# Index scores summed from the PSUM bank of their logits, and a bisection step written as a tensor-scalar operation

## The chip, the cores and the metric

The kernel runs on one core of one Trainium2 chip. The metric is device microseconds (us) of one execution, as the median of several runs. Engines are named as the profile names them: PE (matmul) and PEld (its weight loads), DVE (VectorE), ACT (ScalarE), POOL (GpSimd), SP (SyncE, which issues most DMAs).

## What is computed

Two blocks follow each other on 1024 tokens of 1024 channels. Block 1 has two layers of a hybrid of a spatial gating unit and a sparse attention; block 2 is a windowed attention with a convolution and a mixture of experts. The change touches the sparse attention of block 1 alone, where each query takes the 256 keys with the largest index score:

```python
logits = jnp.einsum('bthd,bsd->bths', qib, k_idx) * (IDX_DIM ** -0.5)     # 8 index heads
score = jnp.einsum('bth,bths->bts', wb, jax.nn.relu(logits)).astype(jnp.float32)
score = jnp.where(causal[None], score, -jnp.inf)
_, idx = lax.top_k(score, top)                                            # top = 256
valid = idx <= qpos[None, :, None]
...
sc = jnp.einsum('bthd,btkd->bthk', qb, k_sel).astype(jnp.float32) * attn_scale
p = jax.nn.softmax(jnp.where(valid[:, :, None, :], sc, -jnp.inf), axis=-1)
```

## The kernel before

The 1024 queries are eight tiles of 128. Tiles 0 and 1 see at most 256 keys and need no choice. For tile i from 2 to 7 the function `select(i)` works on n = 128 (i + 1) keys and writes a bias of 0 or -1e30 for each query and key, which the attention adds to its logits. It has these stages:

- **Scores** (lines 622 to 638). For each of the 8 index heads, and for each of one or two parts of w_ = 384, 512, 320 or 448 keys, PE computes the logits with two matmuls into a PSUM bank of the kind "sm" (L629), ACT rectifies and scales them into an SBUF tile `rel` (L632), and DVE multiplies by the head's weight and adds to the scores `sc` in SBUF (L635 for the first head, L637 for the others). That is 80 such pieces in each layer, 160 in all.
- **Bisection** (L646 to L665). The upper halves of the scores are taken as 16-bit integers `up`. In 15 steps the threshold `cand`, one number for each partition, is found: a count of the keys at or above it (L607), a comparison of the count with K (L662), and the new threshold (L664).
- **Choice** (L668 to L721): lower halves of the scores, ties, and the bias.

Two streams of such tiles run beside each other: (2, 4, 6) and (3, 5, 7). So in each layer there are three bursts of scores, of tiles 2 and 3, of 4 and 5, and of 6 and 7, with bisections between and behind them. They are generators that `bg` places between the steps of the dense products, which keep PE busy meanwhile (the columns for v, u, q, z_a and z_b; `dense_nat`, L100 to L102). What is emitted is put in order by the Tile scheduler, which gives each engine one fixed queue. The queues are worked off strictly in that order, so an instruction that waits holds everything behind it on its engine.

Where tiles live matters here. The bank plan in this stage gives the kind "sm" two PSUM banks, which index logits, the spatial gating products and others take in turn. `rel` has the tag "r2" of the SBUF pool `tmp`, which has seven places that `rel` shares with `up`, `junk`, `lw`, `eq`, `pre` and parts of the modulation rows. A place or a bank is given again when the last reader of its old content is done.

Other work in these stages that the prediction speaks of: the weights of the dense products are split into a high part by ACT (L108, `whi`) and a low part by POOL (L111, `wlo`); POOL also normalizes v for the spatial gate (L798, L799: one multiplication and one addition for each tile of tokens, both with two SBUF inputs) and applies the rotary embedding (L518 to L523). The modulation rows are summed on DVE (L465).

Of the kernel before, what the change touches and what calls it, by code (L numbers as in the profile page):

```python
# [10 lines left out]
FT = mybir.dt.float32  # L11
# [8 lines left out]
OP = mybir.AluOpType  # L20
# [8 lines left out]
BIG = 1e30  # L29
SL = 96          # tokens of one expert's block  # L30
NE = 32
PSUM = bass.MemoryType.PSUM
# [8 lines left out]
def tile_hybrid(ctx, tc, I, out):  # L41
# [7 lines left out]
    banks = {}  # L49
    psum2 = ctx.enter_context(tc.tile_pool(name="psum2", bufs=2, space=PSUM))  # L50

    def bank_plan(big, half, sm, tr, sc=0):
        """Banks of PSUM: big tiles of two, the others of one. Two small and two transposed ones stay in place."""
        if banks:
            banks["stack"].close()
        st = ExitStack()
        banks.update(stack=st, pool=st.enter_context(tc.tile_pool(name="psum", bufs=2, space=PSUM)),
                     big=big, half=half, sm=sm, tr=tr, sc=sc, turn={"sm": 0, "tr": 0})
# [54 lines left out]
    # weights are streamed two 128-row blocks at a time and split one step ahead of their use  # L113
# [11 lines left out]
    # the number of stages whose loads wait for an instruction, and which  # L125
# [33 lines left out]
    # background work, placed between the steps of a product. Generators in bgs yield about the time they take.  # L159
    # Streams hold the vector engine's long chains: they yield the time they take there and whether what comes next  # L160
    # starts on the tensor engine, which then must not come up before the chain is done. now is the tensor engine's
    # time so far, dve that up to which the vector engine has work.
# [97 lines left out]
    def dense_T1(KT, rhs, evac, bgt=1300.0):  # L260
        """One block of 128 channels: the halves take turns so that two banks last."""
# [29 lines left out]
    # every streamed weight, in the order of use  # L291
# [20 lines left out]
    # ------------------------------------------------------------------ block 1  # L312
# [9 lines left out]
    # rotary tables  # L322
# [29 lines left out]
    # modulation rows  # L352
# [13 lines left out]
    # first layer: scale and shift as columns, and h straight into its transposed halves. The products for 256 channels  # L366
    # of one of them are summed over row blocks by the vector engine, by the two slow ones or by the tensor engine.
# [77 lines left out]
    # later modulation rows: products summed over row blocks by the vector engine, over rows by one product with ones  # L445
# [63 lines left out]
    def rope(dst, src, t, H, eng):  # L509
        """Rotary embedding of H heads of 64 channels; t is one tile, or None for all tiles with one head each."""  # L510
# [48 lines left out]
    def layer(l, xin, hT=None):  # L559
# [6 lines left out]
        # keys, values, index keys and index weights  # L566
# [22 lines left out]
        # index queries  # L589
# [20 lines left out]
        def select(i):  # L610
            """Bias of query tile i: 0 at its 256 largest index scores, first ones on ties, else -BIG."""
# [11 lines left out]
            for g in range(2):  # L623
                for j in range(4):
                    h = 2 * j + g
                    for p in range(npart):
# [4 lines left out]
                        rel = tmp.tile([128, 512], FT, name="rel", tag="r2", bufs=7)  # L631
# [10 lines left out]
            # upper halves of the scores as integers: they rise with the scores where these are non-negative and fall  # L642
            # where they are negative. With fewer than 256 non-negative scores the threshold is the (n - 255)-th from the
            # most negative one, and all non-negative ones count as larger.
# [14 lines left out]
            for b in range(14, -1, -1):  # L659
# [4 lines left out]
                V.scalar_tensor_tensor(c2, x, 2.0 ** (b - 1) if b else 0.0, cand, op0=OP.add, op1=OP.add)  # L664
                cand = c2  # L665
                yield 360.0 + .52 * n, False, 0.0, 0.0
            # lower halves of the scores that share the threshold's upper half; of these the K2-th largest, if among the
            # eight largest  # L668
# [29 lines left out]
        def choose(sc, gt, c, cand, z, eq=None, pre=None):  # L698
            """The 256 scores above the threshold with halves cand and c, first ones where equal."""
# [24 lines left out]
        def recheck(tiles):  # L724
            """Tiles with a threshold beyond the eight largest lower halves: these by bisection."""
# [38 lines left out]
        # spatial gating: v, u  # L764
# [7 lines left out]
        def sgu():  # L772
# [3 lines left out]
            # causal spatial weights, transposed  # L776
# [53 lines left out]
        # a unit's probabilities take one place of 1024, or two where there are more than 512 keys  # L830
# [88 lines left out]
        # queries  # L919
# [11 lines left out]
        # z_a: X = 2 * u * spatial gate * silu(z_a)  # L931
# [10 lines left out]
        # z_b, transposed  # L942
# [25 lines left out]
        # half the gate over alpha, and the weights of the output product  # L968
# [49 lines left out]
        def fin2(t, ya, yb, rt):  # L1018
# [11 lines left out]
            # the norm of alpha * x + gate * y, all over alpha  # L1030
# [66 lines left out]
    # ------------------------------------------------------------------ block 2  # L1097
# [53 lines left out]
    def kv_prep():  # L1151
        """Values in two parts; keys with RMS norm and rotary embedding, doubled in X[:, :, 1, 256:512], transposed."""
# [135 lines left out]
    # short convolution on transposed channels  # L1288
# [31 lines left out]
    # gated merge, transposed: M = (1 + tanh) * projection, summed over both branches  # L1320
# [55 lines left out]
    # residual, second norm, router logits  # L1376
# [15 lines left out]
    # routing of one tile of tokens at a time: the two experts of each token, their gates, and the place of each  # L1392
    # assignment in its expert's list; assignment (k, token) is row 1024 k + token of Y
# [36 lines left out]
    def route(t, lg):  # L1430
# [45 lines left out]
        # gates  # L1476
# [7 lines left out]
        # slot + 1 in two exact parts, gate in three exact parts  # L1484
# [294 lines left out]
```

## Time and profile before

| | |
|---|---|
| median of 3 runs | 2515.39 us (2513.58 to 2515.87) |
| span of the profiled execution | 2515.2 us |
| busy: PE, PEld | 2194.3 us (87%), 1914.9 us (76%) |
| busy: DVE | 1705.0 us (68%) |
| busy: ACT, POOL | 1035.8 us (41%), 1301.4 us (52%) |
| scores and bisection of layer 1 | from 132 to about 500 us |
| scores and bisection of layer 2 | from 807 to about 1140 us |

The profile is of one execution, and the page gives its span, from the first instruction to the last; the metric's median is 0.2 us longer than it. The shares of busy time are averages over stages with different limits. The two stretches in the last rows are where the changed lines run, and they are read by themselves below. A duration is that of one instruction on its engine, and it includes what the instruction waits once it has begun; idle time before an instruction is shown with what ended it. "PEclk" is the clock granted to PE, 1.00 being the upper of its two levels.

### The profile page before, as it was taken

How to read it: one execution, taken by the hardware profiler on the slowest of the kernel's cores; microseconds unless marked ns; L12 is line 12 of the kernel's file. 1: busy time of each engine (PE TensorE's matmuls, PEld its weight loads, DVE VectorE, ACT ScalarE, POOL GpSimd, SP SyncE). 2: the span in 40 equal slices, each digit the busy share in tenths (PEclk: the TensorE clock that was granted, in tenths of full speed). 3: DMA queues.
4: the chain of work that ended last, by engine and by line, in shares of the span. 5: the costliest groups of instructions: out<-in, count | busy, mean ns of one | idle time of the engine just before them, and what ended most of it. 6: DMA issues, size and time to landing. Idle time of an engine off the chain costs nothing. (4 is left out here: it accounts for less than half of the span.)

```text
span 2515.2 us, 36403 instructions
## 1 busy us (share of the span) xinstructions
PE 2194.3 (87%) x13235; PEld 1914.9 (76%) x13235; DVE 1705.0 (68%) x3475; ACT 1035.8 (41%) x1875; POOL 1301.4 (52%) x1102
## 2 busy tenths in 40 slices
PE   5997888699989898877998999999998977887885
PEld 5897886488779898766786988888886767776774
DVE  8689889877745879896786268730103357887885
ACT  4233333455532342435564346631212125554554
POOL 4755473456737525725553355432335137776775
PEclk9998999699999899988999999999999989998998
DMA  7522112211123111122211111121211649887893
GB/s 225 181 79 80 50 34 75 90 55 64 39 72 112 37 53 36 58 88 73 73 42 42 39 38 30 30 79 50 64 46 53 234 169 300 265 293 248 272 292 62
DMA packets 146509, 265.51 MB, mean 106 GB/s; under 512 B 23672, under 2 KB 100880, under 8 KB 134016
## 3 DMA queue, kind: packets, MB, share of 16 engines
q1 hardware_dynamic: 139136, 241.99, 29.6%
q0 software_dynamic: 7168, 20.98, 4.0%
q8 instruction: 105, 1.72, 0.3%
q14 instruction: 100, 0.82, 0.1%
HBM read 228.83 MB, written 38.29 MB: 106 GB/s over the span
## 5 line engine op out<-in xcount | busy, mean ns | idle before, releaser
L111 POOL TENSOR_TENSOR wlo<-wraw,whi 128x512 fp32r<-128x512 f32 (+1 forms) x188 | 254.3, 1353 | 490.8 <-ACT whi L108 472.8
L101 PE MATMUL big<-wlo,s 128*128 128x256 f32 (+1 forms) x1536 | 441.2, 289 | 12.8 <-POOL wlo L111 12.8
L100 PE MATMUL big<-whi,s 128*128 128x256 f32 (+1 forms) x1536 | 439.2, 289 | 11.4 <-ACT s L506 8.8
L102 PE MATMUL big<-whi,s 128*128 128x256 f32 (+1 forms) x1536 | 440.9, 289 | 0.0
L101 PEld LDWEIGHTS big<-wlo,s 128*128 128x128 f32 x1536 | 300.1, 196 | 17.8 <-POOL wlo L111 15.2
L100 PEld LDWEIGHTS big<-whi,s 128*128 128x128 f32 x1536 | 296.7, 195 | 18.9 <-ACT s L506 11.2
L102 PEld LDWEIGHTS big<-whi,s 128*128 128x128 f32 x1536 | 299.5, 195 | 2.8 <-issue 0.9
L108 ACT ACTIVATE whi<-wraw 128x512 fp32r<-128x512 f32 (+1 forms) x188 | 117.8, 628 | 419.6 <-PE big L102 143.4
L111 DVE TENSOR_TENSOR ew<-s,ew 128x1024 fp32r<-128x1024 f32 x91 | 209.1, 2321 | 16.9 <-POOL ew L106 9.6
L607 DVE TENSOR_SCALAR_CACHE_REDUCE junk<-up,cand 128x512 bf16<-128x512 int16 (+5 forms) x192 | 179.7, 936 | 1.4
L101 PE MATMUL sm<-ew,xT 128*96 128x256 f32 x512 | 153.8, 300 | 30.3 <-DVE ew L111 25.1
L637 DVE SCALAR_TENSOR_TENSOR s<-rel,widx,s 128x384 f32<-128x384 f32 (+3 forms) x140 | 132.4, 970 | 50.6 <-ACT rel L632 49.9
L102 PE MATMUL sm<-ew,xT 128*96 128x256 f32 x512 | 152.6, 298 | 4.2 <-DVE xT L1627 3.6
L100 PE MATMUL sm<-ew,xT 128*96 128x256 f32 x512 | 152.8, 299 | 0.5 <-ACT ew L108 0.5
L100 PE MATMUL half<-s,whi 128*128 128x512 f32 x320 | 133.1, 416 | 17.9 <-DVE s L950 11.0
L632 ACT ACTIVATE rel<-sm 128x384 f32<-128x384 f32 (+3 forms) x160 | 80.9, 524 | 159.6 <-PE sm L629 105.7
L111 POOL TENSOR_TENSOR ew<-s,ew 128x1024 fp32r<-128x1024 f32 x47 | 130.9, 2792 | 25.3 <-ACT ew L108 18.8
L101 PE MATMUL half<-s,whi 128*128 128x512 f32 x320 | 131.5, 411 | 0.0
L102 PE MATMUL half<-s,wlo 128*128 128x512 f32 x320 | 129.9, 410 | 0.3 <-POOL wlo L111 0.3
L108 ACT ACTIVATE ew<-s 128x1024 fp32r<-128x1024 f32 x116 | 115.5, 1049 | 22.5 <-PE sm L102 11.5
L101 PEld LDWEIGHTS sm<-ew,xT 128*96 128x96 f32 x512 | 89.9, 176 | 40.6 <-DVE ew L111 32.3
L862 POOL TENSOR_SCALAR Z<-Z,rc 128x128 f32<-128x128 f32 (+7 forms) x88 | 63.2, 730 | 109.1 <-DVE rc L860 74.6
(628 smaller groups left out, 6306.9 us busy)
## 6 DMA issues: line engine op xcount, KB each, us to landing
wraw<-in_w_in_dram SPq DMA_DIRECT2D x164, 256.0 KB, 2.9
adaw<-in_w_ada_dram SPq DMA_DIRECT2D x48, 512.0 KB, 4.1
s<-in_w_gate_e_dram SPq DMA_DIRECT2D x23, 1024.0 KB, 4.8
s<-in_w_up_e_dram SPq DMA_DIRECT2D x23, 1024.0 KB, 7.2
s<-in_w_down_e_dram SPq DMA_DIRECT2D x23, 1024.0 KB, 9.2
X<-in_w_gate_e_dram SPq DMA_DIRECT2D x9, 1024.0 KB, 6.7
X<-in_w_up_e_dram SPq DMA_DIRECT2D x9, 1024.0 KB, 6.8
X<-in_w_down_e_dram SPq DMA_DIRECT2D x9, 1024.0 KB, 8.6
```

What stands on the lines that cost most here:

```text
L100: T.matmul(o, lh, rh, start=start, stop=False, skip_group_check=True)
L101: T.matmul(o, lh, rl, start=False, stop=False, skip_group_check=True)
L102: T.matmul(o, ll, rh, start=False, stop=stop, skip_group_check=True)
L108: A.activation(hi, src, AF.Copy)
L111: return (sub or V).tensor_tensor(lo, src, hi.bitcast(FT), op=OP.subtract)
L607: V.tensor_scalar(junk[:, :src.shape[1]], src, thr, 0.0, op0=op, op1=OP.add, accum_out=cnt)
L632: A.activation(rel[:, :w_], ps[:, :w_], AF.Relu, scale=0.125)
L637: V.scalar_tensor_tensor(d, rel[:, :w_], widx[:, i, h:h + 1], d, op0=OP.mult, op1=OP.add)
L862: G.tensor_scalar(P[hh][:, :n], P[hh][:, :n], rc[:, hh:hh + 1], 1.0, op0=OP.mult, op1=OP.mult)
```

## The change

Two lines of `select` are changed. All else in the diff are comments and docstrings that fall away, with blank lines in their place, so that the line numbers stay.

```diff
                             T.matmul(ps[:, :w_], qT[g][:, j, :], kist[a][:, p * w_:(p + 1) * w_], start=a == 0,
                                      stop=a == 1)
-                        rel = tmp.tile([128, 512], FT, name="rel", tag="r2", bufs=7)
+                        rel = ps
                         A.activation(rel[:, :w_], ps[:, :w_], AF.Relu, scale=0.125)
                         d = sc[:, p * w_:(p + 1) * w_]
...
                 V.tensor_scalar(x, cnt, K[:, 0:1], -float(2 ** b), op0=OP.is_lt, op1=OP.mult)
                 c2 = small1.tile([128, 1], FT, name=f"cand{z}")
-                V.scalar_tensor_tensor(c2, x, 2.0 ** (b - 1) if b else 0.0, cand, op0=OP.add, op1=OP.add)
+                V.tensor_scalar(c2, x, 2.0 ** (b - 1) if b else 0.0, cand[:, 0:1], op0=OP.add, op1=OP.add)
                 cand = c2
```

With the first, ACT writes the rectified logits over the logits in their PSUM bank, and DVE reads them there (L635, L637); `rel` takes no SBUF place any more, and the bank is given again only when DVE has read it. With the second, the old threshold enters as a scalar for each partition instead of a second tensor of one element; the arithmetic is the same.

Since buffers decide when the scheduler may place an instruction, the queues are ordered anew. Three places:

POOL in layer 1, around the normalization of v, before (`wlo` are low parts of weights that the dense product waits for, `X` the values of v, `vg` the gain and bias):

```order
L111 TENSOR_TENSOR wlo_2923<-wraw_2920,whi_2922 128x512
L798 TENSOR_TENSOR X_79<-X_79,vg_2756 128x512 x8
L799 TENSOR_TENSOR X_79<-X_79,vg_2756 128x512 x2
L781 AFFINE_SELECT ws_2761<-ws_2761 128x1024
L799 TENSOR_TENSOR X_79<-X_79,vg_2756 128x512
L111 TENSOR_TENSOR wlo_3136<-wraw_3133,whi_3135 128x512
```

and in the changed kernel:

```order
L111 TENSOR_TENSOR wlo_2875<-wraw_2872,whi_2874 128x512
L798 TENSOR_TENSOR X_79<-X_79,vg_2708 128x512 x8
L111 TENSOR_TENSOR wlo_3088<-wraw_3085,whi_3087 128x512
L799 TENSOR_TENSOR X_79<-X_79,vg_2708 128x512 x2
L781 AFFINE_SELECT ws_2713<-ws_2713 128x1024
```

The next low part of weights stands directly behind the eight multiplications now, ahead of three additions and the masking of the spatial weights.

PE in layer 1, at the end of the burst of tiles 4 and 5, before (`sm` are the logits' banks, `kist` the index keys, `qT` the index queries, `big` a dense product):

```order
L629 MATMUL sm_2603<-kist0_767,qT1_2377 128x384
L629 MATMUL sm_2603<-kist1_768,qT1_2377 128x384
L100 MATMUL big_3132<-whi_3273,s32_225 128x256
L101 MATMUL big_3132<-wlo_3274,s32_225 128x256
L102 MATMUL big_3132<-whi_3273,s32_226 128x256
L100 MATMUL big_3132<-whi_3273,s32_225 128x256
```

and in the changed kernel:

```order
L629 MATMUL sm_2504<-kist0_767,qT1_2361 128x384
L629 MATMUL sm_2504<-kist1_768,qT1_2361 128x384
L629 MATMUL sm_2509<-kist0_767,qT1_2330 128x320
L629 MATMUL sm_2509<-kist1_768,qT1_2330 128x320
L629 MATMUL sm_2514<-kist0_767,qT1_2361 128x384
L629 MATMUL sm_2514<-kist1_768,qT1_2361 128x384
```

Ten pieces of logits follow each other with nothing between them at this place now; before, dense matmuls stood between most of them.

DVE in layer 1, at the start of the burst of tiles 6 and 7, before (`s4` are the scores, `eq`, `pre`, `bias` the choice of tile 5):

```order
L710 TENSOR_SCALAR need1_3542<-cnt1_3540 128x1
L716 SCALAR_TENSOR_TENSOR pre_3563<-ones_102,eq_3562 128x768
L635 TENSOR_SCALAR s4_3667<-rel_3726,widx_816 128x448
L635 TENSOR_SCALAR s4_3667<-rel_3744,widx_816 128x448
L718 TENSOR_SCALAR pre_3563<-pre_3563,need1_3542 128x768
L719 TENSOR_TENSOR eq_3562<-eq_3562,pre_3563 128x768
```

and in the changed kernel:

```order
L710 TENSOR_SCALAR need0_3364<-cnt0_3362 128x1
L716 SCALAR_TENSOR_TENSOR pre_3399<-ones_102,eq_3398 128x640
L635 TENSOR_SCALAR s4_3619<-sm_3675,widx_816 128x448
L607 TENSOR_SCALAR junk_1212,cnt1_3379<-up_2631,cand1_3341 128x768
L635 TENSOR_SCALAR s4_3619<-sm_3692,widx_816 128x448
L718 TENSOR_SCALAR pre_3399<-pre_3399,need0_3364 128x640
```

The first scores of tile 6 are summed earlier in DVE's queue now, beside the choice of tile 4, while tile 5 is still being bisected.

## Rows read from the trace of the kernel before

**Rows 1.** The page: the span, and busy time of each engine with its share of the span and its instructions.

```profile
span 2515.2 us, 36403 instructions
PE 2194.3 (87%) x13235; PEld 1914.9 (76%) x13235; DVE 1705.0 (68%) x3475; ACT 1035.8 (41%) x1875; POOL 1301.4 (52%) x1102
```

**Rows 2.** Windows: start and end of a stretch, its length, then the busy time of PE, PEld, DVE, ACT and POOL in it with their instructions, the granted PE clock, the DMA share and GB/s.

```profile
160.00:222.00 62.00, 56.93 (x438) 53.01 (x438) 61.84 (x214) 16.82 (x28) 14.75 (x11) 0.94 0.39 111
222.00:250.00 28.00, 20.52 (x140) 18.53 (x138) 27.96 (x28) 12.22 (x25) 27.07 (x16) 0.86 0.21 57
278.00:341.00 63.00, 53.37 (x395) 50.98 (x395) 62.73 (x174) 14.38 (x25) 29.93 (x32) 0.97 0.14 37
409.00:500.00 91.00, 64.65 (x262) 49.96 (x260) 81.53 (x214) 36.48 (x88) 40.36 (x43) 0.74 0.27 88
836.00:896.00 60.00, 45.33 (x345) 43.39 (x344) 59.61 (x202) 20.71 (x38) 33.11 (x26) 0.89 0.15 41
905.00:936.00 31.00, 31.00 (x249) 31.00 (x248) 18.56 (x40) 13.36 (x28) 6.62 (x6) 1.00 0.18 47
1061.00:1140.00 79.00, 53.93 (x231) 42.23 (x231) 72.89 (x190) 28.14 (x69) 30.96 (x36) 0.78 0.28 87
```

**Rows 3.** Groups by line over the whole span: count, busy us and mean ns of one, then the idle time of the engine just before them and what ended it.

```profile
L637 DVE SCALAR_TENSOR_TENSOR s<-rel,widx,s 128x384 f32<-128x384 f32 (+3 forms) x140 | 132.4, 970 | 50.6 <-ACT rel L632 49.9
L632 ACT ACTIVATE rel<-sm 128x384 f32<-128x384 f32 (+3 forms) x160 | 80.9, 524 | 159.6 <-PE sm L629 105.7 <-DVE lw L695 23.3 <-DVE s L635 10.6
L664 DVE SCALAR_TENSOR_TENSOR cand<-xb,cand 128x1 f32<-128x1 f32 x180 | 60.9, 338 | 1.6
```

**Rows 4.** Timeline of DVE from 868.6 us, in a bisection of layer 2, and the row of POOL at that time: start, us, instruction.

```profile
868.62 0.20 DVE L662 TENSOR_SCALAR xb<-cnt,K 128x1 f32<-128x1 f32 x1
869.27 0.64 DVE L664 SCALAR_TENSOR_TENSOR cand<-xb,cand 128x1 f32<-128x1 f32 x1
...
867.41 4.92 POOL L798 TENSOR_TENSOR X<-X,vg 128x512 f32<-128x512 f32 x4
```

**Rows 5.** All instructions of four lines: duration in ns as minimum, median and maximum, first and last start in us, shapes.

```profile
L662 DVE TENSOR_SCALAR xb<-cnt,K x180: 180/206/217, 163.6 to 1117.7; 128x1 f32<-128x1 f32 x180
L664 DVE SCALAR_TENSOR_TENSOR cand<-xb,cand x180: 115/158/1240, 164.8 to 1118.0; 128x1 f32<-128x1 f32 x180
L430 DVE TENSOR_SCALAR yT<-tr,cols x10: 794/800/812, 27.9 to 67.0; 128x512 f32<-128x512 f32 x10
L637 DVE SCALAR_TENSOR_TENSOR s<-rel,widx,s x140: 533/774/1859, 137.4 to 1059.9; 128x384 f32<-128x384 f32 x42, 128x512 f32<-128x512 f32 x42, 128x320 f32<-128x320 f32 x28, 128x448 f32<-128x448 f32 x28
```

**Rows 6.** Windows of line L664 alone: stretch, length, DVE's busy time in that line with its count, then clock, DMA share and GB/s.

```profile
278.00:341.00 63.00, 11.43 (x29) 0.97 0.14 37
380.00:409.00 29.00, 3.74 (x10) 0.89 0.27 73
836.00:896.00 60.00, 13.11 (x30) 0.89 0.15 41
936.00:998.00 62.00, 8.88 (x27) 1.00 0.15 41
1019.00:1061.00 42.00, 5.57 (x11) 0.96 0.20 62
```

**Rows 7.** Timeline of POOL from 222.9 us and of DVE at 237.6 us (layer 1, tiles 4 and 5); then POOL in the same work of layer 2, while DVE bisects.

```profile
222.93 5.09 POOL L111 TENSOR_TENSOR wlo<-wraw,whi 128x512 fp32r<-128x512 f32 x1 [12.87 <-ACT whi L108]
227.97 12.34 POOL L798 TENSOR_TENSOR X<-X,vg 128x512 f32<-128x512 f32 x8
246.12 1.60 POOL L111 TENSOR_TENSOR wlo<-wraw,whi 128x512 fp32r<-128x512 f32 x1
237.62 11.99 DVE L637 SCALAR_TENSOR_TENSOR s<-rel,widx,s 128x320 f32<-128x320 f32 x8
...
866.19 1.26 POOL L799 TENSOR_TENSOR X<-X,vg 128x512 f32<-128x512 f32 x1
```

**Rows 8.** Timeline of DVE in layer 1: two sums of 512 keys. The last row is a group by shape, from 0 to 1300 us: the spatial gate's product (L816), an operation of the same kind whose first input lies in PSUM; columns as in Rows 3.

```profile
388.53 0.75 DVE L637 SCALAR_TENSOR_TENSOR s<-rel,widx,s 128x512 f32<-128x512 f32 x1
389.32 1.66 DVE L637 SCALAR_TENSOR_TENSOR s<-rel,widx,s 128x512 f32<-128x512 f32 x1
L816 DVE SCALAR_TENSOR_TENSOR X<-sm,bs,X 128x512 f32<-128x512 f32 x16 | 11.8, 740 | 0.0
```

**Rows 9.** Windows of line L637 alone, columns as in Rows 6.

```profile
341.00:360.00 19.00, 12.24 (x11) 1.00 0.11 29
380.00:409.00 29.00, 10.36 (x10) 0.89 0.27 73
1024.00:1061.00 37.00, 13.23 (x14) 0.95 0.23 70
```

**Rows 10.** Timeline of PE at 137.4 us: two dense matmuls that follow each other.

```profile
137.41 0.28 PE L102 MATMUL big<-whi,s 128*128 128x256 f32 x1
137.53 0.29 PE L100 MATMUL big<-whi,s 128*128 128x256 f32 x1
```

**Rows 11.** Timelines of PE, ACT and DVE around 333 us (layer 1, start of the burst of tiles 6 and 7) and around 1050 us (layer 2, its end).

```profile
333.28 0.68 PE L629 MATMUL sm<-kist,qT 128*128 128x448 f32 x2 [3.53 <-ACT rel L632]
332.68 1.07 ACT L632 ACTIVATE rel<-sm 128x448 f32<-128x448 f32 x2 [6.37 <-DVE eq L719]
341.51 0.78 DVE L635 TENSOR_SCALAR s<-rel,widx 128x448 f32<-128x448 f32 x2
...
1046.78 1.46 PE L629 MATMUL sm<-kist,qT 128*128 128x512 f32 x4
1056.24 0.75 DVE L637 SCALAR_TENSOR_TENSOR s<-rel,widx,s 128x512 f32<-128x512 f32 x1
```

**Rows 12.** All instructions of line L635, columns as in Rows 5.

```profile
L635 DVE TENSOR_SCALAR s<-rel,widx x20: 368/954/4180, 133.1 to 1026.3; 128x384 f32<-128x384 f32 x6, 128x512 f32<-128x512 f32 x6, 128x320 f32<-128x320 f32 x4, 128x448 f32<-128x448 f32 x4
```

## The prediction

> **What bounds the kernel now.** I read the page first, then windows of the two stretches in which the changed lines run, then the groups by line, then timelines at places where a duration looked odd. The page makes PE the busiest engine by far [rows 1]. The windows say otherwise for the stretches in question [rows 2]: from 160 to 222, 278 to 341 and 836 to 896 us DVE is busy for all but 0.2, 0.3 and 0.4 us, while PE has 5 to 15 us to spare. At the end of each selection, 409 to 500 and 1061 to 1140 us, PE idles 26 and 25 us at a clock of 0.74 and 0.78: the attention of the last tiles waits for their bias. So in each layer it is DVE's chain (scores, bisection, choice, three times over) that sets when the attention can finish, and a microsecond taken off that chain moves the end, as long as PE keeps its 25 us of room.
>
> What makes DVE slow shows in durations. The new threshold, one number for each partition, takes 338 ns on average, its neighbour L662, also one number, has a median of 206 ns and stays between 180 and 217; L664 goes from 115 to 1240 [rows 3, 5]. In the timeline L664 takes 0.64 us while POOL runs its multiplications, and L662 0.20 beside the same work [rows 4]. L664 reads two tensors from SBUF and L662 one. The sums L637 have the same trouble: 0.75 us alone, 1.66 us with POOL at work [rows 8], 970 ns on average [rows 3]. From 237.6 to 249.6 us eight of them took 1.50 us each, and POOL's eight multiplications just before and beside them 1.54 each, where POOL's additions beside the bisection took 1.26 [rows 7]. The two engines take turns instruction by instruction.
>
> **The change, part by part.**
>
> *Bisection.* 180 operations lose their second tensor. I price the new one like L662, 206 ns: one tensor input, one pointer scalar, an immediate. Saved by stretch (busy time less count times 0.206) [rows 6]: 11.43 - 5.97 = 5.5; 3.74 - 2.06 = 1.7; 13.11 - 6.18 = 6.9; 8.88 - 5.56 = 3.3; 5.57 - 2.27 = 3.3. Sum **-20.7 us**, all on DVE where it is full or nearly so; the rest of the 180 run where there is less to gain. Bounds: 0, if the new form waits like the old, and -23.8 (60.9 - 180 x 0.206, [rows 3]) if all counts. Alone the new form is slower than the old (206 against a median of 158), so where POOL is quiet it costs 0.05 us a step; the stretch sums contain that.
>
> *Sums from PSUM.* No operation of the trace reads `rel` in PSUM. The nearest row is L816, the same kind of operation with a PSUM and an SBUF tensor and a pointer scalar: 740 ns at 512 elements, and no more than L637's undisturbed 0.75 [rows 8]. So I take the undisturbed price: 0.75 at 512, and from L637's minimum of 0.53 over all lengths [rows 5] an estimate of 0.6 to 0.7 for the shorter ones. The worst bound is today's mean. For L635, which has one input, the nearest PSUM row is L430 with 800 ns [rows 5], against 368 to 4180 today [rows 12]; its sum is about even, and I count it as nothing. What is gained counts only where DVE runs without gaps:
> - 222 to 250 us: POOL's run from 222.9 to 247.7 would be near 17 us at 1.26 each instead of 25 [rows 7], and in the new order the low part of weights stands ahead of three additions. PE had 7.5 us of idle time there [rows 2], which caps it: -6.
> - 341 to 360: 12.24 against 11 x 0.69 = 7.6; half of the 4.6 counted, as DVE waits for PE right after: -2.3. 380 to 409: 10.36 - 10 x 0.74 = -3.0.  1024 to 1061: 13.23 - 14 x 0.74 = -2.9 [rows 9].
>
> Sum **-14.2 us**, bounds 0 and -41 (all 140 at an undisturbed mean of 0.65: 132.4 - 91 [rows 3]). [...]
>
> *ACT.* L632 writes to PSUM instead of SBUF, 160 times 524 ns [rows 3]. No row shows that; the nearest are its own. From half to double would be 40 us less or 80 more on an engine that idles over half of these windows [rows 2], and 0.5 us more in a bank's cycle. I count nothing. The 23.3 us for which ACT waited until `lw` freed an SBUF place [rows 3] vanish, but DVE was then behind anyway (ACT resumed at 332.7, DVE came to that piece at 341.5 [rows 11]), so this moves nothing but the order.
>
> *The bank held longer.* A bank was free after two matmuls and L632, about 0.6 + 0.6 us; now after L637 too, about 2.0 us at 512, so with two banks at most one piece a microsecond. The order shows the answer: more dense matmuls between the pieces. From the first to the sixteenth piece of the first burst stand 207 dense matmuls, 172 before; at the end of the same burst of layer 2 the last piece has 42 more ahead of it than before, and at the end of layer 2's second burst 62 more. A dense matmul takes 0.12 us start to start [rows 10]. DVE idles in such a burst (18.56 of 31 us busy while PE is at 31.00, from 905 to 936 [rows 2]), so a longer burst lengthens its chain: 35 x 0.12 = 4.2, 42 x 0.12 = 5.0, 62 x 0.12 = 7.4, **+16.6 us**. For the second burst of layer 1 I count nothing, as its last piece stands behind the same dense matmul as before; for the third bursts neither: they end 36 and 24 matmuls later on PE (4.3 and 2.9 us), but DVE was 9 to 10 us behind PE at that end [rows 11], which two banks forbid now.
>
> Sum: -20.7 - 14.2 + 16.6 = -18.3. The span is 2515.2 us, the median 2515.4, so **2497 us**, 0.7% less.
>
> **Rivals.**
> - *PE stands at the bank* (slower). PE reached the third piece of the third burst at 333.3 us, and DVE took the first one, whose bank that piece would need now, until about 341.9 [rows 11]: 8.6 us for which PE, and the dense products queued behind, would stand. Over six bursts such delays of DVE behind PE sum to some 46 us, at most 10.2 in one place (1046.8 against 1057.0, [rows 11]). The new order moves the third piece forward, 64 dense matmuls (7.7 us) behind the second and not 139, so DVE's lead must come from the gains before it. If all 46 fell on the path: -35 + 17 + 46 = +28, 2543 us; half, 2520. It decides if DVE comes to a burst later than PE by more than the gains give back. For it: the dense products carry PE's room. Against: that room, and a scheduler that knows of the banks.
> - *The bursts cost nothing* (faster still): PE runs ahead, DVE's waits in bursts shrink, and the 16.6 falls away: 2515.4 - 35 = 2480.
> - *A wash*: what the bisection gains is idled away in the next burst, since PE's order sets when pieces come. 2513, within 0.2% of before (5 us, about what a measurement of this kernel can tell from no change).
> - *The new threshold waits too.* L635, a tensor-scalar operation with one SBUF input, took between 368 ns and 4.18 us [rows 12]. If L664 became like it, the first term is 0: -14.2 + 16.6 = +2, 2518. [...] Against it stands L662's maximum of 217 ns over 180 executions, many beside POOL [rows 5].
>
> **How the numbers follow.** My forecast has 0.45, with a range of its own from 2486 to 2508 (terms off by half); the free bursts 0.17; a wash 0.10; the waiting threshold 0.04; PE at the bank 0.24, of which a little falls within 0.2%. Faster by over 0.2%: 0.62; within: 0.16; slower: 0.22. The range must leave out no more than 2 in 10: it reaches down to 2466, between the free bursts and the bound of the sums, and up to 2532, where half of the bank's case is in.
>
> **What would show it.** L664 at 206 ns without a tail; L637 near 0.65 us on average, none over 1 us; POOL's run of layer 1 some 7 us shorter; the idle time of PE before L629 up, now put down to DVE's L637; the bias of tile 7 some 10 us earlier in each layer, and the same attention behind it. I am wrong if L637 stays near 970 ns, if PE's idle time between 130 and 410 us grows by more than 10 us, or if the time is outside the range.

## The result, and the profile after

| | before | after |
|---|---|---|
| median of the runs, us | 2514.48 (4 runs, 2512.94 to 2515.87) | 2530.08 (4 runs, 2523.55 to 2534.58) |
| span of the profiled execution, us | 2515.2 | 2527.6 |
| start of the second block (first L1223), us | 1469.8 | 1470.8 |
| first gather of the experts (L1604), us | 2064.9 | 2066.0 |
| from there to the end, us | 450.3 | 461.6 |

The changed kernel takes 1.0066 times as long (95% interval 1.0054 to 1.0079). Measured again beside the experiments it took 2538.0 against 2513.2, a ratio of 1.0101 (1.0077 to 1.0124). It is slower, where faster was forecast. Below, one execution is left out of a median: the profiled one of the kernel that writes to a 'tr' bank, which took 2580.8 us at a granted clock of 0.82 where the others of that kernel had 0.94, so that only its times are read.

TensorE is PE, VectorE DVE, ScalarE ACT. The first L1223 stands for the start of block 2, and a gather fetches the tokens of an expert.

The two edits shortened their own operations as the prediction said. The page of the profile after, against [rows 1]:

```profile
span 2527.6 us, 36368 instructions
PE 2216.7 (88%) x13235; PEld 1924.7 (76%) x13235; DVE 1632.5 (65%) x3475; ACT 1037.7 (41%) x1875; POOL 1267.3 (50%) x1102
```

DVE works 72.5 us less, and the time is longer. The groups by line of after, columns as in [rows 3]:

```profile
L637 DVE SCALAR_TENSOR_TENSOR s<-sm,widx,s 128x384 f32<-128x384 f32 (+3 forms) x140 | 90.4, 654 | 95.0 <-ACT sm L632 94.4
L632 ACT ACTIVATE sm<-sm 128x384 f32<-128x384 f32 (+3 forms) x160 | 80.4, 508 | 184.9 <-PE sm L629 176.1 <-DVE s L637 3.2 <-DVE thr L704 3.1
L664 DVE TENSOR_SCALAR cand<-xb,cand 128x1 f32<-128x1 f32 x180 | 37.6, 209 | 1.3
L629 PE MATMUL sm<-kist,qT 128*128 128x384 f32 (+3 forms) x320 | 94.5, 386 | 37.0 <-DVE s L635 19.9 <-DVE s L637 15.9 <-DVE X L816 0.8
```

L637 went from 970 to 654 ns and L664 from 338 to 209. But VectorE's idle time before L637 went from 50.6 to 95.0 us, and ScalarE's waiting for the products of L629 from 105.7 to 176.1 [rows 3]: the pieces come later. TensorE now waits before L629 for VectorE (37.0 us); before, it waited for ScalarE, and less (13.8):

```profile
L629 PE MATMUL sm<-kist,qT 128*128 128x384 f32 (+3 forms) x320 | 89.2, 369 | 13.8 <-ACT rel L632 12.5 <-DVE X L816 1.2
```

(the same row of before). All instructions of three lines of after, columns as in [rows 5]; the tails of [rows 5, 12] are gone:

```profile
L664 DVE TENSOR_SCALAR cand<-xb,cand x180: 184/209/218, 164.0 to 1119.9; 128x1 f32<-128x1 f32 x180
L637 DVE SCALAR_TENSOR_TENSOR s<-sm,widx,s x140: 539/636/754, 133.8 to 1070.8; 128x384 f32<-128x384 f32 x42, 128x512 f32<-128x512 f32 x42, 128x320 f32<-128x320 f32 x28, 128x448 f32<-128x448 f32 x28
L635 DVE TENSOR_SCALAR s<-sm,widx x20: 521/636/753, 133.0 to 1034.0; 128x384 f32<-128x384 f32 x6, 128x512 f32<-128x512 f32 x6, 128x320 f32<-128x320 f32 x4, 128x448 f32<-128x448 f32 x4
```

Where the time went shows in windows (columns as in [rows 2]) from the first index product to the second block, and from the first gather to the end. Before:

```profile
132.10:1469.80 1337.70, 1172.87 (x7489) 1045.56 (x7488) 1020.02 (x2369) 558.28 (x1061) 691.95 (x630) 0.93 0.20 61
2064.90:2515.20 450.30, 346.55 (x2240) 300.26 (x2240) 347.20 (x300) 233.33 (x319) 317.12 (x160) 0.90 0.79 247
```

After:

```profile
132.00:1470.80 1338.80, 1186.61 (x7488) 1051.81 (x7487) 956.29 (x2369) 559.85 (x1061) 668.20 (x630) 0.92 0.20 61
2066.00:2527.60 461.60, 355.87 (x2240) 304.74 (x2240) 339.18 (x300) 233.79 (x319) 306.64 (x160) 0.88 0.78 241
```

Two separate things are to be seen. In the first block, 64 us less work of VectorE changed the length by 1.1 us: TensorE idles 12.6 us less (length less busy time, 164.8 and 152.2), and the same matmuls take 13.7 us more. And 11.3 of the 12.4 us by which the spans differ arise among the experts, which the change does not edit.

### The profile page after: what moved, and what is told of

Same layout as the page of the kernel before. It is cut to its first block, busy times and chain, and to the rows that moved or that the text cites. A ratio compares the mean times of both kernels' runs of the same rounds, so it can differ in the third digit from the quotient of the medians.

```text
span 2527.6 us, 36368 instructions
## 1 busy us (share of the span) xinstructions
PE 2216.7 (88%) x13235; PEld 1924.7 (76%) x13235; DVE 1632.5 (65%) x3475; ACT 1037.7 (41%) x1875; POOL 1267.3 (50%) x1102
## 5 line engine op out<-in xcount | busy, mean ns | idle before, releaser
L111 POOL TENSOR_TENSOR wlo<-wraw,whi 128x512 fp32r<-128x512 f32 (+1 forms) x188 | 246.5, 1311 | 532.9 <-ACT whi L108 507.9
L101 PE MATMUL big<-wlo,s 128*128 128x256 f32 (+1 forms) x1536 | 441.5, 289 | 9.3 <-POOL wlo L111 9.3
L100 PE MATMUL big<-whi,s 128*128 128x256 f32 (+1 forms) x1536 | 439.1, 290 | 10.1 <-ACT s L506 6.8
L102 PE MATMUL big<-whi,s 128*128 128x256 f32 (+1 forms) x1536 | 440.5, 288 | 0.2 <-DVE s L507 0.2
L101 PEld LDWEIGHTS big<-wlo,s 128*128 128x128 f32 x1536 | 299.8, 195 | 15.1 <-POOL wlo L111 11.4
L100 PEld LDWEIGHTS big<-whi,s 128*128 128x128 f32 x1536 | 297.3, 195 | 18.1 <-ACT s L506 9.5
L102 PEld LDWEIGHTS big<-whi,s 128*128 128x128 f32 x1536 | 299.2, 195 | 2.1 <-DVE s L507 0.4
L111 DVE TENSOR_TENSOR ew<-s,ew 128x1024 fp32r<-128x1024 f32 x91 | 184.7, 2051 | 41.0 <-POOL ew L106 22.4
L101 PE MATMUL sm<-ew,xT 128*96 128x256 f32 x512 | 153.3, 299 | 29.7 <-DVE ew L111 16.2
L632 ACT ACTIVATE sm<-sm 128x384 f32<-128x384 f32 (+3 forms) x160 | 80.4, 508 | 184.9 <-PE sm L629 176.1
L102 PE MATMUL sm<-ew,xT 128*96 128x256 f32 x512 | 150.8, 294 | 3.8 <-DVE xT L1627 3.5
L100 PE MATMUL sm<-ew,xT 128*96 128x256 f32 x512 | 151.4, 296 | 0.8 <-ACT xT L1626 0.8
L637 DVE SCALAR_TENSOR_TENSOR s<-sm,widx,s 128x384 f32<-128x384 f32 (+3 forms) x140 | 90.4, 654 | 95.0 <-ACT sm L632 94.4
L108 ACT ACTIVATE ew<-s 128x1024 fp32r<-128x1024 f32 x116 | 116.5, 1050 | 40.8 <-PE big L102 18.0
L100 PE MATMUL half<-s,whi 128*128 128x512 f32 x320 | 130.2, 407 | 2.3 <-ACT X L1120 1.7
L101 PE MATMUL half<-s,whi 128*128 128x512 f32 x320 | 129.4, 404 | 0.0
L102 PE MATMUL half<-s,wlo 128*128 128x512 f32 x320 | 128.2, 404 | 0.2 <-POOL wlo L111 0.2
L629 PE MATMUL sm<-kist,qT 128*128 128x384 f32 (+3 forms) x320 | 94.5, 386 | 37.0 <-DVE s L635 19.9
L101 PEld LDWEIGHTS sm<-ew,xT 128*96 128x96 f32 x512 | 88.5, 173 | 40.9 <-DVE ew L111 22.6
```

The source lines that it names most:

```text
L100: T.matmul(o, lh, rh, start=start, stop=False, skip_group_check=True)
L101: T.matmul(o, lh, rl, start=False, stop=False, skip_group_check=True)
L102: T.matmul(o, ll, rh, start=False, stop=stop, skip_group_check=True)
L108: A.activation(hi, src, AF.Copy)
L111: return (sub or V).tensor_tensor(lo, src, hi.bitcast(FT), op=OP.subtract)
L629: T.matmul(ps[:, :w_], qT[g][:, j, :], kist[a][:, p * w_:(p + 1) * w_], start=a == 0, stop=a == 1)
```

## The experiments

Two theories for the first block. **Bank**: the edit of `rel` costs in the bursts what both edits save, because a bank is held longer; it can do so by making TensorE stand (WAIT) or by the order that the scheduler then writes (ORDER). Against it, **not on the path**: VectorE's chain has room, and neither edit moves the end. For the experts: **order**, the one that the scheduler writes anew there, against **state**: how the transfers fall in those executions, whatever the order. In the built program the experts' instructions of the changed kernel stand in another order on PE, ACT, DVE and POOL from about the eighth expert on (SP's order is the same).

To hold an order, a table of places is read, and consecutive instructions of an engine are chained without a wait:

```
for a, b in zip(want, want[1:]):
    tc.add_manual_dep(b, a.name, nosync, reason="order")
```

In such kernels line numbers are shifted. Each experiment was timed in at least 6 runs beside the kernel before, whose medians lay between 2513.2 and 2515.6. L1223 and the other places in time are those of one profiled execution; where the first block stands in the same order in several kernels, L1223 differs by up to 3 us (1469.8 and 1466.8 with the order of before).

**One edit alone.** First the candidate:

```
-V.scalar_tensor_tensor(c2, x, ..., cand, op0=OP.add, op1=OP.add)
+V.tensor_scalar(c2, x, ..., cand[:, 0:1], op0=OP.add, op1=OP.add)
```

> Only the candidate edit (L664 with the candidate as a per-partition scalar); the rectified logits go to SBUF as before. In this build the experts' instructions stand in the same order as in the kernel before. Theory BANK (the edit of rel costs in the bursts what both edits save; VectorE's chain does set the end of the first block): the 180 candidate updates fall from 338 to about 209 ns mean, the first instruction of the second block (L1223) comes 10 to 21 us earlier than 1469.8 us and the time is 2494 to 2505 us. Rival NOT ON THE PATH (the chain has room, so neither edit moves the end): the updates fall as much, L1223 stays within 3 us of 1469.8, time 2512 to 2518 us.

Measured: 2486.8 us, ratio 0.9889 (0.9864 to 0.9913); L1223 at 1442.2, 27.5 us earlier. The operations lost 23.3 us. The windows of that kernel, and its group L637:

```profile
131.20:1442.20 1311.00, 1162.42 (x7487) 1034.32 (x7487) 1006.36 (x2369) 557.76 (x1061) 698.47 (x630) 0.95 0.21 63
2038.40:2479.50 441.10, 347.67 (x2240) 301.37 (x2240) 340.38 (x300) 233.04 (x318) 320.08 (x160) 0.90 0.81 253
```

```profile
L637 DVE SCALAR_TENSOR_TENSOR s<-rel,widx,s 128x384 f32<-128x384 f32 (+3 forms) x140 | 134.6, 990 | 44.9 <-ACT rel L632 44.5
```

The end of the block moves, so "not on the path" is out. The gain is over what was expected at best: TensorE idles 16 us less and its matmuls also take 10 us less. The scheduler rewrites the order for this edit too (2291 matmuls in the six bursts against 2294 before, so little in the bursts), and no run has the edit in the old order: how much the shorter operation does alone is not shown. From `rel` alone, the next kernel, to both edits L1223 moves by about as much, 25.6 us (1496.4 and 1470.8). Then `rel` alone:

```
-rel = tmp.tile([128, 512], FT, name="rel", tag="r2", bufs=7)
+rel = ps
```

> Only the edit of rel (logits rectified in their PSUM bank and summed from there); candidate updates as before. The experts' instructions are held in the order that they have in the kernel before, so that only the first two blocks differ. Theory BANK: L637 about 0.66 us mean, but L1223 comes 10 to 22 us later than 1469.8, time 2525 to 2537 us. Rival NOT ON THE PATH: L1223 within 3 us of 1469.8, time 2512 to 2518 us. A third, that this edit alone gains what its shorter operations save: L1223 10 us earlier, time about 2505 us.

Measured: 2540.8, ratio 1.0100 (1.0074 to 1.0126); L1223 at 1496.4, 26.7 us later; time and L1223 lie 4 to 5 us beyond the range for BANK. L637 took 653 ns.

**Wait or order.** Both edits, but all engines in the order of the kernel with the candidate edit alone:

> Both edits, rectified logits in their bank, but all engines work in the order of the kernel with the candidate edit alone. Theory ORDER: nothing is lost, and L637 is shorter: L1223 at 1425 to 1443 us, time 2470 to 2488 us. Theory WAIT: the in-order TensorE now meets the held banks earlier and stands there: L1223 at 1460 us or later, time 2505 us or more.

Measured: 2485.4, ratio 0.9891 (0.9862 to 0.9919); L1223 at 1438.8. Both lie in the ranges for ORDER. The 32 us against the changed kernel are gone, with the banks held until VectorE has read, as there. Two groups and the window of that kernel (L1012 is L629, L1020 is L637):

```profile
L1012 PE MATMUL sm<-kist,qT 128*128 128x384 f32 (+3 forms) x320 | 90.8, 374 | 32.7 <-DVE s L1018 22.3 <-DVE s L1020 10.0 <-DVE X L1199 0.4
L1020 DVE SCALAR_TENSOR_TENSOR s<-sm,widx,s 128x384 f32<-128x384 f32 (+3 forms) x140 | 89.6, 654 | 87.5 <-ACT sm L1015 86.7
```

```profile
132.20:1438.80 1306.60, 1162.07 (x7488) 1034.99 (x7487) 949.74 (x2369) 557.69 (x1061) 668.61 (x630) 0.94 0.20 63
```

TensorE stands at the banks here too, 32.7 us against 37.0, and the kernel is fast all the same: WAIT is out. Next, only TensorE's instructions between the first and the last index product of each of the six bursts held in that order, with the rest left to the scheduler, which writes it anew around them:

> The changed kernel, both edits, experts in the order of the kernel before; of the first two blocks only TensorE's instructions inside the six bursts (from the first to the last product of index scores of a burst) are held in the order that the kernel with the candidate edit alone has there, everything else is left to the scheduler. Theory ORDER IN THE BURSTS (the 294 products more that stand between the pieces are the loss): L1223 at 1436 to 1450 us, time 2482 to 2500 us. Rival ORDER ELSEWHERE (the attention or the bisections lose it): L1223 at 1460 to 1475, time 2508 to 2522 us.

Measured: 2493.9, ratio 0.9919 (0.9895 to 0.9943); L1223 at 1440.6, both in the ranges for the order in the bursts. So TensorE's order inside the bursts is enough to bring back 30 of the 32 us. Windows of the bursts, with TensorE's matmuls counted (the first number in brackets): the first two of layer 2 and the sum over all six, before,

```profile
806.38:833.85 27.47, 27.47 (x210) 26.77 (x209) 17.66 (x18) 12.14 (x24) 20.44 (x24) 1.00 0.17 47
861.11:937.80 76.69, 62.02 (x466) 60.08 (x465) 61.39 (x156) 30.13 (x61) 34.42 (x28) 0.91 0.16 43
...
sum 356.99, PE 319.80 PEld 305.33 DVE 296.88 ACT 139.58 POOL 234.72; mean PE 53.30 PEld 50.89 DVE 49.48 ACT 23.26 POOL 39.12
```

after,

```profile
808.04:840.90 32.86, 32.86 (x255) 32.17 (x254) 14.08 (x30) 14.15 (x26) 18.18 (x24) 1.00 0.18 47
846.87:953.54 106.67, 89.71 (x659) 86.57 (x657) 77.29 (x245) 36.83 (x71) 41.26 (x33) 0.90 0.15 41
...
sum 414.04, PE 369.49 PEld 348.21 DVE 290.42 ACT 151.59 POOL 228.66; mean PE 61.58 PEld 58.03 DVE 48.40 ACT 25.27 POOL 38.11
```

and with the bursts held:

```profile
838.02:919.66 81.64, 64.61 (x466) 62.65 (x465) 58.15 (x160) 30.53 (x61) 34.29 (x28) 0.87 0.15 41
...
sum 357.65, PE 318.93 PEld 304.47 DVE 255.22 ACT 141.09 POOL 211.66; mean PE 53.16 PEld 50.74 DVE 42.54 ACT 23.52 POOL 35.28
```

The scheduler put 293 matmuls more between the pieces (the six counts sum to 2587 and 2294), 193 of them in the second burst of layer 2, and the bursts grew by 57 us. Those products are not extra work, they are only done earlier, so a part of it comes back later. Their number is therefore no measure of the loss. In the second burst of layer 2, some 150 of the 193 stand in one gap: after its first two pieces, which come early, 216 matmuls pass before the third; in the held kernel 68.

```profile
846.87 0.83 PE L629 MATMUL sm<-kist,qT 128*128 128x320 f32 x4
...
891.92 0.90 PE L629 MATMUL sm<-kist,qT 128*128 128x320 f32 x2 [7.55 <-DVE s L635]
```

The loss lies mostly elsewhere. Of the 30 us, 24 are lost between the first index product of layer 1 and that of layer 2, and 14.9 of these in the third burst of layer 1, with 36 matmuls more, 11.8 us more of TensorE's busy time, and a lower clock. After:

```profile
132.00:808.04 676.04, 598.88 (x3736) 527.30 (x3735) 488.96 (x1204) 277.52 (x523) 354.89 (x328) 0.91 0.23 69
309.99:406.99 97.00, 84.98 (x543) 77.81 (x542) 71.71 (x159) 32.46 (x58) 58.89 (x68) 0.91 0.15 41
```

and held:

```profile
131.20:783.28 652.08, 580.49 (x3736) 512.32 (x3735) 485.93 (x1204) 276.97 (x523) 355.65 (x328) 0.95 0.24 71
302.97:385.07 82.10, 73.21 (x507) 68.57 (x506) 65.52 (x146) 31.02 (x55) 57.80 (x67) 0.96 0.14 38
```

The window of the whole first block in the held kernel:

```profile
131.20:1440.60 1309.40, 1160.18 (x7488) 1033.43 (x7487) 952.67 (x2369) 558.06 (x1061) 668.93 (x630) 0.95 0.21 63
```

Against after, TensorE idles only 3.0 us less (149.2 and 152.2), but its matmuls take 26.4 us less, at a granted clock of 0.95 and not 0.92. The loss thus shows as the same matmuls at a lower granted clock, hardly as longer idling. What lowers the clock was not separated.

The reverse: candidate edit alone, but TensorE and ScalarE in the changed kernel's order up to the experts:

> The candidate edit alone (rectified logits in SBUF), but in the first two blocks TensorE and ScalarE work in the order that they have in the changed kernel, where more products stand between the pieces of the bursts; the experts' instructions in the order of the kernel before. Theory ORDER (the loss of the edit of rel is the order that the scheduler writes when banks are held longer): L1223 at 1458 to 1475 us, time 2503 to 2520 us, against 1442.3 and 2487 with its own order. Theory WAIT (the loss is the wait of TensorE at the held bank while the kernel runs): L1223 at 1438 to 1450 us, time 2483 to 2496 us.

Measured: 2563.1, ratio 1.0193 (1.0168 to 1.0218); L1223 at 1517.3, far beyond both ranges. That order costs the SBUF version 75 us, more than the 32 that it costs with the rectified logits in PSUM; its sums took 0.95 us each and not 0.65. So with this order of TensorE and ScalarE the edit of `rel` is worth 46.5 us (1470.8 against 1517.3; VectorE's and GpSimd's orders differ between the two), and 3.4 in the other order (1438.8 against 1442.2), which is no more than the scatter. That the order matters is confirmed; why it costs the SBUF version so much more stays open.

**More banks.** The logits take the 'sm' and the 'tr' banks in turn, both edits, experts held in the order of before (as in the next two and in `rel` alone):

```
-ps = bank([128, 512], "sm")
+ps = bank([128, 512], turn[next(turns) % 2])     # ("sm", "tr")
```

> Both edits, and the pieces' logits take the two 'sm' and the two 'tr' banks in turn, so that four pieces can be between TensorE and VectorE instead of two; the experts' instructions are held in the order of the kernel before. Theory BANK (two banks, now held until VectorE has read, are what eats the gain): the bursts shorten again (last piece of the last burst of the second layer before 1050 us instead of 1071.6), the second block starts (L1223) at 1430 to 1450 us instead of 1470.8, time 2478 to 2500 us. Rival PORT (PSUM is the slower place whatever the number of banks, or VectorE's waits for ScalarE, not the banks): L1223 at 1462 to 1480 us, time 2508 to 2528 us. It can also lose, if the transposes of the attention that use the 'tr' banks come to wait: then above 2528 us.

Measured: 2485.1, ratio 0.9875 (0.9850 to 0.9900); L1223 at 1433.2, all in the ranges for BANK; the last piece of layer 2 is summed by 984.3, 76 us before its time in the kernel before. With banks to spare the scheduler writes short bursts (233 us in sum). The same with `rel` in SBUF:

> The candidate edit and the four banks in turn for the logits, but the rectified logits go to SBUF as in the kernel before; the experts' instructions in the order of the kernel before. It tells what the edit of rel is worth once banks are plenty, against the four-bank kernel with both edits (2485, L1223 at 1433.2). If summing from PSUM gives its shorter operations back to the end: L1223 10 to 20 us later, 1443 to 1455 us, time 2492 to 2505 us, since banks were not what the SBUF version waited for (candidate edit alone: 1442.3). If the four banks alone are the gain: L1223 at 1425 to 1437 us, time 2477 to 2489 us.

Measured: 2507.9, ratio 0.9975 (0.9955 to 0.9995); L1223 at 1463.1, worse than both expectations: the four banks alone lose 21 us against the candidate edit alone, though the last piece of layer 2 comes 27 us earlier (1010.3 against 1037.0). Scores that are done sooner are thus not enough by themselves. ScalarE writing to a 'tr' bank:

```
-rel = ps
+rel = bank([128, 512], "tr")
```

> Both edits, but ScalarE writes the rectified logits into a bank of the 'tr' pair instead of back into their own, so that the logits' 'sm' bank is free when ScalarE has read it, as in the kernel before, and VectorE still sums from PSUM; the experts' instructions are held in the order of the kernel before. Theory BANK: most of the loss goes, since TensorE waits for ScalarE alone, while VectorE's operations stay at about 0.65 us: L1223 at 1432 to 1455 us, time 2480 to 2505 us; ScalarE may now wait at the 'tr' bank. Rival PORT: as in the four-bank kernel, 2508 to 2528 us.

Measured: 2504.2, ratio 0.9949 (0.9928 to 0.9970), at the upper end of the range for BANK: 16 us less than the changed kernel with the experts in the same order (2520.4, below), so about half of the loss and not most of it. And four banks with no order held:

> The kernel with both edits and four banks in turn, with no order held anywhere, the experts' neither: the version that could be used as it stands. L1223 at 1433 us as in the one with the experts held; its experts' order is its own, which may cost or save 10 us: 2475 to 2500 us. If over 2505 us, the order that the scheduler writes for the experts decides over the gain of the first block.

Measured: 2496.3, ratio 0.9938 (0.9924 to 0.9952); L1223 at 1427.7, the experts 459.4 us. It starts the second block 5.5 us earlier than the kernel with the experts held, where they took 447.0 us, and by the medians ends 11 us later.

**The experts.** Only the order of the experts' instructions exchanged: the changed kernel with that of before, and the kernel before with that of the change.

> The changed kernel, both edits, every instruction of the first two blocks in the same order as there; the experts' instructions, which the change does not edit, are held on each engine in the order that they have in the kernel before. Theory ORDER (11 of the 12 us come from the order that the scheduler wrote for the experts): from the first gather (L1604) to the end 449 to 453 us instead of 461.6, time 2514 to 2519 us, the same as before within 0.2%. Rival STATE (the loss comes from how the transfers fall in these executions, whatever the order): 458 to 464 us from the first gather, time 2526 to 2533 us.

> The kernel before, neither edit, its first two blocks in its own order; the experts' instructions are held in the order that they have in the changed kernel. Theory ORDER: from the first gather to the end 458 to 464 us instead of 450.3, time 2523 to 2531 us, slower than before by about 0.5% with neither edit in it. Rival STATE: 449 to 453 us, time 2513 to 2518 us.

Measured: the first 2520.4 (12 runs, 2513.4 to 2528.5), ratio 1.0013 (0.9995 to 1.0032); the second 2534.0, ratio 1.0064 (1.0042 to 1.0087); both 1 to 3 us above the ranges for ORDER; STATE is 6 and 16 us off. The second is clear: all its runs lie from 2525.1 to 2536.2, so the order of instructions that nobody edited makes the kernel before as slow as the changed one was. The first is less so. Its 12 runs fall in two groups, six from 2513.4 to 2516.8 and six from 2523.9 to 2528.5, and the median lies in the gap between them; the profiled execution is of the upper group and has 459.3 us from the gather to the end, as STATE expected. So with the experts' old order the loss is gone in half of the executions, and on average the change then makes no difference clear of noise. What sets the two groups apart is not known. Then the changed kernel again:

> The changed kernel once more, beside the two kernels of this call and the kernel before, to have its experts a second time: by theory ORDER of the experts they take 457 to 470 us from the first gather (L1604) to the end, the 128x512 products of L100 to L102 about 460 ns mean as in the changed kernel and in the kernel before with the experts' order of the change (461 and 461; with the order of before 428 and 443), time 2522 to 2536 us. If the loss was the state of those executions, 441 to 453 us and 2512 to 2518.

Measured: 2538.0, ratio 1.0101 (1.0077 to 1.0124), experts 470.2; the time is 2 us beyond the range for ORDER. Over these profiles the experts took 441.2 to 459.5 us in the order of before (nine kernels, one profile each), and 461.6, 469.3 and 470.2 in that of the change. The order decides on average; within one order some 18 us of scatter remain, over kernels whose first blocks differ. The group of the experts' second product, in the kernel before, the changed kernel, and the kernel before with the experts' order of the change (where L172 is L100):

```profile
L100 PE MATMUL big<-ew,hdT 128*96 128x512 f32 x128 | 54.9, 429 | 10.8 <-ACT ew L108 9.5 <-ACT hdT L1650 1.3
```

```profile
L100 PE MATMUL big<-ew,hdT 128*96 128x512 f32 x128 | 59.3, 463 | 2.2 <-ACT hdT L1650 1.3 <-ACT yt L1663 0.9
```

```profile
L172 PE MATMUL big<-ew,hdT 128*96 128x512 f32 x128 | 59.4, 464 | 2.2 <-ACT hdT L1722 1.3 <-ACT yt L1735 0.9
```

With L101 and L102 it is 177.1 us after and 164.4 before, 12.7 more: again the same matmuls at a lower clock (0.88 and 0.90 in the windows above), while over the whole of the experts TensorE idles 2 us more. What lowers it stays open.

## Why the prediction was wrong, point by point

The time lay in the range and on the wrong side: 15.6 us slower by the medians, where 18.3 faster was forecast. The ledger by L1223 and, for the experts, by the time from the first gather to the end, each term from one pair of kernels:

| term | predicted | measured | from |
|---|---|---|---|
| bisection | -20.7 | -27.5 | candidate edit alone, against before |
| sums from PSUM | -14.2 | -3.4 | both edits in that kernel's order, against it |
| bank held longer | +16.6 | +32.0 | changed kernel, against the one just named |
| experts | none | +11.3, +19.9 | two profiles of the changed kernel, against before |

The first three measured terms add up to +1.1 us, which but for rounding is what L1223 moved by (1.0). Three steps failed: the credit for the sums, the size of the bank's term, and the experts, which were put at nothing.

- *Bisection*: right, and rather too small. L664 took 209 ns against 206, 218 at most. The premise, that VectorE's chain sets the end, held for this term, as far as two pairs of kernels show whose orders also differ (27.5 and 25.6 us). That the new L664 would wait as L635 did [rows 12], as a rival had it, shows in none of its executions (184 to 218 ns).
- *Sums from PSUM*: the price was right (654 ns against 0.65 us), the credit was not: **the first step that failed**, -3.4 us against -14.2, and 3 us are scatter. "Counts only where DVE runs without gaps" was the rule, but the gaps open once the sums are shorter. In an unchanged order the sums took 45.0 us less (134.6 and 89.6), and VectorE waited 42.6 us longer for ScalarE before them (44.9 and 87.5). Pieces come at the pace of the engines before it, so what a sum saves goes into waiting for the next piece. At its minimum L637 took 533 ns from SBUF [rows 5] and 539 from PSUM. One reading of the prediction was wrong: the 0.75 us of [rows 8] is not L637 alone, for POOL was at work beside both sums there; as a price it held (754 ns at most).

```profile
387.37 3.06 POOL L937 TENSOR_TENSOR X<-X,s 128x512 f32<-128x512 f32 x2
```

- *ACT*: right to be counted as nothing, 508 ns against 524.
- *The bank held longer*: **the second step that failed, and the largest in the first block**. The mechanism was right, the order that the scheduler writes in the bursts, but it was priced at 0.12 us for each dense matmul by which the last piece of three bursts moved back: 139 of them, 16.6 us, 12.4 of them in layer 2. The cost is 32 us, and with the bursts held 24 of the 30 us that come back do so in layer 1. The third bursts were put at nothing because VectorE was behind TensorE there; the third burst of layer 1 alone takes 14.9 us more than in the held order, 4.3 of them for 36 dense matmuls at 0.12. The rest is a price that the prediction does not have: the same matmuls at a lower clock (0.91 against 0.96 in that burst), and 3 us of idle time.
- *The end of the sum*: **the third step that failed**. The sum stopped where the edited code stops, and so put the experts at nothing; they took 11.3 and 19.9 us more. That the scheduler would write them anew was to be seen in the built program, and no case of the prediction has it. By the medians it is the larger part of the slowdown; with the experts' old order the change is a wash (1.0013), in the median of two groups of runs.
- *Rivals*: TensorE does stand at the bank, 23 us more, but in the kernel that gains 31 us it stands nearly as long. "A wash" came nearest for the first block, in time and in half of its reason: TensorE's order sets when the pieces come, but what is idled away is the saving of the sums, while that of the bisection reached the end where it stood alone.
- *What would show it*: L664, L637 and the idle time before L629 came as said, though that is put down to L635 (19.9 us) more than to L637 (15.9). The bias of tile 7 did not come 10 us earlier: 488.7 against 491.0, and 1140.0 against 1136.4. The run of POOL was to be 7 us shorter; its eight multiplications took 11.47 us against 12.34 [rows 7]:

```profile
229.36 11.47 POOL L798 TENSOR_TENSOR X<-X,vg 128x512 f32<-128x512 f32 x8 [11.19 <-DMA vg<-in_v_norm_g_dram]
```

TensorE's idle time between 130 and 410 us fell, from 36.8 to 25.5, so this condition for being wrong was not met (before, then after):

```profile
130.00:410.00 280.00, 243.17 (x1713) 226.21 (x1712) 253.24 (x563) 97.44 (x180) 154.90 (x140) 0.94 0.23 63
130.00:410.00 280.00, 254.52 (x1744) 233.54 (x1744) 212.12 (x563) 98.46 (x182) 138.04 (x141) 0.93 0.22 63
```

How an order can cost time shows in one place of after: from 884 to 892 us TensorE is busy for 0.45 us while it stands before a piece (the one at 891.92 above, 7.55 us put down to L635), and the products queued behind, L102 and L100, start only after it, at 892.62 and 892.84 us.

```profile
884.00:892.00 8.00, 0.45 (x5) 0.25 (x3) 8.00 (x25) 2.15 (x5) 4.20 (x3) 0.71 0.13 34
```

## What to carry to other kernels

When a scheduler writes the order, a change can act through the order as much as through its operations (here 32 us against 27.5): compare the whole built order, also of the parts not edited, and ask what moved there. Counting the instructions that moved does not price it: 193 of 293 stood where little was lost. A shorter operation is worth its saving only where its input is already waiting; where another engine paces the pieces, it becomes idle time (here 42.6 of 45.0 us). The old order only avoided the loss here (-3.4 us from the shorter sums); with four banks the kernel with sums from PSUM is 30 us ahead of that with sums from SBUF (1433.2 and 1463.1), each in its own order. Judge each edit by itself: here one of the two alone makes the kernel 1.1% faster (0.9889), and the other alone 1.0% slower (1.0100).

## What the runs showed that was not expected

- The same 7,488 matmuls of the first block keep TensorE busy for 1160 to 1187 us, at a granted clock of 0.95 and 0.92, depending on small moves in the order. In the bursts' order alone that was 26.4 us, against 3.0 us of idle time.
- Within one order of the experts, their time scatters from 441 to 460 us over nine kernels; in two executions of the changed kernel it was 461.6 and 470.2.
- With an SBUF operand less the whole tail was gone: L637 up to 1859 ns before [rows 5], 754 after; L664 up to 1240 before [rows 5], 218 after.
